# A unit of dense work between the two parts of the second row's scores in stick-breaking attention

## The chip, the cores and the metric

The program runs on one core of a Trainium2 chip. The metric is the device time of one execution in microseconds (us). A core has five engines with queues of their own: TensorE (PE, with its weight loads listed apart as PEld), VectorE (DVE), ScalarE (ACT), GpSimd (POOL) and SyncE (SP), which issues the DMAs here. Each runs its instructions in the order in which they stand, and waits on semaphores for what another engine or a DMA has to deliver.

## The reference

Two layers of a decoder on 1024 tokens of width 1024. Each layer has a mixer of two branches, an output projection and a gated FFN with a short convolution. Branch B of the mixer is the place of the change: strictly causal stick-breaking attention, four heads of 64, swept over blocks of 128 queries.

```python
def block(args):
    q_blk, i = args
    z = jnp.einsum('bhqc,bhkc->bhqk', q_blk, kt).astype(jnp.float32) * scale
    qpos = i * BLOCK + jnp.arange(BLOCK)
    causal = key_pos[None, :] < qpos[:, None]
    log_stay = jnp.where(causal, jax.nn.log_sigmoid(-z), 0.0)
    later = lax.cumsum(log_stay, axis=3, reverse=True) - log_stay
    attn = jnp.where(causal, jnp.exp(jax.nn.log_sigmoid(z) + later), 0.0)
    return jnp.einsum('bhqk,bhkc->bhqc', attn, vt)
...
for l in range(DEPTH):
    h = rmsnorm(x, norm1[l])
    proj = h @ w_in[l]
    ...
    o_a = dilated_mixture(...)
    o_b = stick_breaking_attention(...)
    gates = jax.nn.sigmoid(gate_pre + b_gate[l])
    merged = g_a * (o_a @ w_br[l, :OUT_A]) + g_b * (o_b @ w_br[l, OUT_A:])
    x = x + merged @ w_o[l]
```

## The kernel before

All large products run in f32 accuracy from two reduced parts of each operand (a high part `hi` made by a cast on ACT, a low part `lo` made by a subtraction on DVE), so that one product is three matmuls. The input projections and the gates are computed in pairs with seven block products instead of eight (`pair`, `seven`). Half of one such block product, six matmuls with 512 columns each (lines 1064 to 1066, twice), is a **unit**: a generator hands out one at each step.

The class `Dense` owns these generators. `step()` issues the next unit, with whatever casts, copies and DMAs belong to it; `advance(rate)` adds a rate to the account `due` and calls `step()` for each whole one in it. The function `attend` walks through the attention of the layer in 16 stick items, 4 near items and 16 far items. For each it issues short attention steps one after the other (scores, transpositions, products with the values) and calls `dense.advance(rate)` after each, so that units of dense work stand between the attention's steps on PE. The scores of the next item are issued between the steps of the current one.

A stick item is one head (`u`, 0 to 3, called a **round** below) and one pair of query blocks (`qp`, 3 down to 0). It has two rows of scores, one for each of the two query blocks: `score(0)` and `score(1)`. A row of L keys is worked in parts of at most 512 columns, the last keys first. For each part, two matmuls (lines 649 and 650) write a PSUM bank `z`, and ACT reads it twice: a sigmoid into `beta` (line 716) and one into `stay` (line 717). POOL masks the diagonal block of a row's first part. The pool of banks for `z` has two banks, used in turn, so the part after next has to wait until ACT has read the part. Behind the second row, `scans(2)` puts running products on DVE (lines 736, 738) and their products with `beta` (line 743). Blocks of `beta` are then transposed by PE (line 751, into `sb_t`), split by ACT and DVE (lines 144 and 151, `sbh` and `sbl`) and multiplied with the values (line 764).

Rows with more than 512 keys have two parts. Of second rows these are the ones of `qp` 3 (512 and 512 columns) and `qp` 2 (512 and 256). In the order on PE, a round has the parts z1 (512 columns) and z2 (384) of the first row of `qp` 3, z3 and z4 (512 each) of its second row, z5 (512) and z6 (128) of the first row of `qp` 2, and later z7 (512) and z8 (256) of its second row. There are four rounds in a layer and two layers.

The order of ACT, DVE, POOL and SP is not that of the code alone. A scheduler orders the instructions by priority (the scores' sigmoids and some others are written under `tc.high_priority`), and manual dependencies without a semaphore keep some of them behind others.

Of the kernel before, what the change touches and what calls it, by code (L numbers as in the profile page):

```python
# [63 lines left out]
def trunk_kernel(ctx, tc, x, norm1, w_in, b_gate, w_br, w_o, norm2, w_up, conv_w, conv_b, w_down, norm_f, out, depth=None, probe=None):  # L64
# [63 lines left out]
    def bank(tag, name):  # L128
        return ps.tile([P, 512], F32, tag=tag, name=name)

    def small(name, dtype=F32):
        return sb.tile([P, 512], dtype, tag="pt", bufs=PT, name=name)
# [358 lines left out]
    def table(func, after):  # L491

        junk = sb.tile([P, 1], F32, tag="junk", name="junk")
        return act.activation(junk, after, func, bias=eps[:, 0:1], scale=0.0)
# [153 lines left out]
    def scores(o, qt, ql, k):  # L648
        pe.matmul(o, qt, k, start=True, stop=False, skip_group_check=True)
        pe.matmul(o, ql, k, start=False, stop=True, skip_group_check=True)  # L650

    def parts(src, n, name):

        hi, lo = small(name + "h", F32R), small(name + "l", F32R)
        with tc.high_priority(offset=AHEAD):
            split(hi[:, :n], lo[:, :n], src[:, :n], "is")
        return hi, lo

    def fold(dst, o):

        n = o.shape[-1]
        tmp = small("fold")
        with tc.high_priority(offset=AHEAD):
            act.copy(tmp[0:64, :n], o[64:128, :])
            dve.tensor_tensor(dst, o[0:64, :], tmp[0:64, :n], ALU.add)
# [33 lines left out]
    def stick_item(dense, u, qp):  # L699
        q, k, v = R["slots"][:, qp], R["kv"][:, 0, :], R["kv"][:, 1, :]  # L700
        pr, s = divmod(u, 2)
        rows, st, shared, left = {}, {}, {}, []

        def score(a):
            L = P * (2 * qp + a + 1)
            bt = rows[a] = sb.tile([P, T], F32, tag="p4", bufs=4, name="beta")
            if a == 0:
                st[0] = sb.tile([P, 2, T], F32, tag="xa", bufs=4, name="stay")
            sv = st[0][:, a, :]
            for c1 in range(L, 0, -512):  # L710
                c0 = max(0, c1 - 512)
                w = c1 - c0
                z = bank("s", "z")
                scores(z[:, :w], *(q[:, x, a * P : a * P + P] for x in range(2)), k[:, c0:c1])
                with tc.high_priority(offset=AHEAD):
                    act.activation(bt[:, c0:c1], z[:, :w], AF.Sigmoid)
                    last = act.activation(sv[:, c0:c1], z[:, :w], AF.Sigmoid, scale=-1.0)
                    if (u, qp, a, c0) == (3, 0, 1, 0):
                        one = table(AF.Exp, zero[:, 0:1])
                        tc.add_manual_dep(one.ins, last.ins.name, NO_SYNC, reason="behind")  # L720
                    if c1 == L:
                        pool.affine_select(bt[:, L - P : L], bt[:, L - P : L], [[-1, P]], ALU.is_gt, 0.0, base=0, channel_multiplier=1)
                (SCANS if c1 == L else left).append((shared, bt, sv, c0, c1, L))
            if a:
                SCANS.extend(left)
                dense.rows += 1
                scans(2)

        def scans(most):

            while SCANS and most:
                most -= 1
                _, bt, sv, c0, c1, L = SCANS.pop(0)
                rev = sv[:, c0:c1][:, ::-1]
                if c1 == L:
                    one = dve.tensor_tensor_scan(rev, rev, over[:, HF - (c1 - c0) : HF][:, ::-1], 1.0, ALU.mult, ALU.max)
                else:
                    one = dve.tensor_tensor_scan(rev, rev, zero[:, 0:1].to_broadcast([P, c1 - c0]), sv[:, c1 : c1 + 1], ALU.mult, ALU.add)
                if "dve" in LAST:
                    tc.add_manual_dep(one.ins, LAST["dve"], NO_SYNC, reason="in turn")  # L740
                k0, k1 = max(0, c0 - 1), c1 - 1
                with tc.high_priority(offset=AHEAD):
                    LAST["mult"] = dve.tensor_tensor(bt[:, k0:k1], bt[:, k0:k1], sv[:, k0 + 1 : k1 + 1], ALU.mult).ins.name

        def turn(kb):
            while any(x[0] is shared and x[4] > kb * P for x in SCANS):
                scans(1)
            tp = bank("t", "sb_t")
            todo = [(j, a) for j in range(2) for a in range(2) if kb + j <= 2 * qp + a]
            for c, (j, a) in enumerate(todo):  # L750
                pe.transpose(tp[:, c * P : c * P + P], rows[a][:, (kb + j) * P : (kb + j + 1) * P], ident)
            shared[kb] = parts(tp, len(todo) * P, "sb")
            scans(2)

        def apply(kb):
            first = kb == 2 * qp
            if first:
                shared["o"] = bank("o", "sb_o")[:, :256]
                dense.free[qp] = u + 1
            o = shared["o"]  # L760
            for j in range(2):
                c = P if first and j else 0
                for p in (0, 1):
                    pe.matmul(
                        o[:, c:256],
                        v[:, (kb + j) * P : (kb + j + 1) * P],
                        shared[kb][p][:, 256 * j : 256 * j + 256 - c],
                        start=(first and j == 0 and p == 0),
                        stop=(kb == 0 and j == 1 and p == 1),
                        skip_group_check=True,  # L770
                    )
            if kb == 0:
                out_ = small("ob")[0:64, 0:256]
                fold(out_, o)
                nc.sync.dma_start(obd[64 * s : 64 * s + 64, pr, qp * 256 : (qp + 1) * 256], out_)

        sc = [lambda: score(0), lambda: score(1)]
        return sc, [(lambda kb=kb: turn(kb), lambda kb=kb: apply(kb)) for kb in range(2 * qp, -2, -2)]

# [1439 lines left out]
```

## Time and profile before

| | |
|---|---|
| Time, median of 3 runs | 2613.97 us (2612.62 to 2614.74) |
| Time of the profiled execution | 2614.89 us |
| Its span, first to last instruction | 2613.2 us |
| PE busy | 2602.9 us (100%) |
| PEld busy | 2181.2 us (83%) |
| DVE busy | 2086.4 us (80%) |
| ACT busy | 1353.4 us (52%) |
| POOL busy | 107.4 us (4%) |
| Stick attention, first layer | about 75 to 330 us |
| Stick attention, second layer | about 1366 to 1620 us |

Matmuls overlap in their pipeline and their ends are modelled, so PE counts as busy while it streams at its full rate and also through a short wait. What a wait costs is read from the distance between the starts of matmuls. A row of the time line has the start in us, the duration in us, the engine, the line, the operation and its tiles; in brackets stands idle time of the engine before it, and what ended it.

### The profile page before, as it was taken

Reading aid. Unit: us, or ns where it says so; the run is one execution under the profiler, and the core shown is the slowest. Engines: PE = TensorE matmul, PEld = TensorE weight load, DVE = VectorE, ACT = ScalarE, POOL = GpSimd, SP = SyncE. Lnnn points to the kernel's source line nnn. Section 1 sums busy time; section 2 is a strip of 40 time slices with the busy share of each in tenths; the row PEclk is TensorE's granted clock in tenths of the full one; section 3 lists DMA queues with packets and bytes.
Section 4 is the critical chain, followed back from the end, with each engine's and each line's share of the span. In section 5 each row is a group of like instructions: output and inputs, shape, how many; then the busy total and the mean of one; then the engine's idle time right before and its main releaser. Section 6 shows DMA issues by size and latency. Waiting matters only on the chain.

```text
span 2613.2 us, 36182 instructions
## 1 busy us (share of the span) xinstructions
PE 2602.9 (100%) x12706; PEld 2181.2 (83%) x12706; DVE 2086.4 (80%) x3486; ACT 1353.4 (52%) x2527; POOL 107.4 (4%) x145
## 2 busy tenths in 40 slices
PE   9999999999999999999999999999999999999999
PEld 8888888888888888888888888888888888888887
DVE  7877777785988888897677788777869888889965
ACT  6555666573554555422345555666645555554225
POOL 3000000030000000000000000000300000000000
PEclk9999999999999999999999999999999999999999
DMA  7534578973244454688344436798633344447962
GB/s 255 152 119 133 161 206 218 235 241 97 89 145 161 137 172 135 241 325 312 145 150 142 129 124 186 199 235 230 200 101 121 121 168 139 154 161 263 347 241 107
DMA packets 401123, 470.36 MB, mean 180 GB/s; under 512 B 24468, under 2 KB 315692, under 8 KB 399148
## 3 DMA queue, kind: packets, MB, share of 16 engines
q1 hardware_dynamic: 400220, 465.90, 55.4%
q0 software_dynamic: 704, 2.13, 0.4%
q8 instruction: 101, 1.65, 0.3%
q14 instruction: 82, 0.67, 0.1%
q10 hardware_dynamic: 16, 0.00, 0.0%
HBM read 305.33 MB, written 162.63 MB: 179 GB/s over the span
## 4 chain that ended last, share of the span: by engine, by line
PE 93%; DVE 3%; DMA 2%; ACT 2%; issue 1%; POOL 0%; DVEq 0%; ACTq 0%; POOLq 0%
PE u_a L1064 6%; PE u_a L1065 6%; PE u_a L1066 6%; PE d_ps L1827 5%; PE d_ps L1829 5%; PE d_ps L1828 5%; PE i_a L1064 5%; PE i_a L1066 5%; PE i_a L1065 5%; PE u_c L1064 3%; PE u_c L1065 3%; PE u_c L1066 3%; PE i_c L1064 2%; PE i_c L1066 2%; PE i_c L1065 2%; PE o_ps L185 2%
## 5 line engine op out<-in xcount | busy, mean ns | idle before, releaser
L144 ACT CAST w_hi<-up_a 128x512 fp32r<-128x512 f32 x280 | 174.1, 623 | 276.8 <-DVE up_a L1681 120.6
L151 DVE TENSOR_TENSOR w_lo<-up_a,w_hi 128x512 fp32r<-128x512 f32 x280 | 189.5, 689 | 83.6 <-ACT w_hi L144 83.6
L144 ACT CAST w_hi<-in_a 128x512 fp32r<-128x512 f32 x252 | 156.2, 622 | 166.6 <-PE i_c L1065 37.8
L151 DVE TENSOR_TENSOR w_lo<-in_a,w_hi 128x512 fp32r<-128x512 f32 x252 | 172.8, 688 | 74.5 <-ACT w_hi L144 65.8
L1835 DVE TENSOR_TENSOR x<-x,d_ps 128x512 f32<-128x512 f32 (+1 forms) x228 | 153.6, 675 | 64.9 <-PE d_ps L1829 61.5
L1827 PE MATMUL d_ps<-gd_in,w_hi 128*128 128x512 f32 (+1 forms) x340 | 130.0, 382 | 0.0
L1828 PE MATMUL d_ps<-gd_in,w_hi 128*128 128x512 f32 (+1 forms) x340 | 129.8, 382 | 0.0
L1829 PE MATMUL d_ps<-gd_in,w_lo 128*128 128x512 f32 (+1 forms) x340 | 129.8, 382 | 0.0
L1064 PE MATMUL u_a<-hh,w_hi 128*128 128x512 f32 x320 | 124.5, 389 | 0.0
L1065 PE MATMUL u_a<-hl,w_hi 128*128 128x512 f32 x320 | 124.5, 389 | 0.0
L1066 PE MATMUL u_a<-hh,w_lo 128*128 128x512 f32 x320 | 124.5, 389 | 0.0
L1064 PE MATMUL u_a<-t_hi,w_hi 128*128 128x512 f32 x320 | 124.5, 389 | 0.0
L1065 PE MATMUL u_a<-t_lo,w_hi 128*128 128x512 f32 x320 | 124.5, 389 | 0.0
L1066 PE MATMUL u_a<-t_hi,w_lo 128*128 128x512 f32 x320 | 124.5, 389 | 0.0
L1064 PE MATMUL i_a<-hh,w_hi 128*128 128x512 f32 x288 | 119.2, 414 | 0.0
L1064 PE MATMUL i_a<-t_hi,w_hi 128*128 128x512 f32 x288 | 118.3, 411 | 0.0
L1827 PE MATMUL d_ps<-gd_in,wd 128*128 128x512 f32 (+1 forms) x292 | 113.9, 390 | 0.0
L1066 PE MATMUL i_a<-hh,w_lo 128*128 128x512 f32 x288 | 113.1, 393 | 0.0
L1066 PE MATMUL i_a<-t_hi,w_lo 128*128 128x512 f32 x288 | 113.0, 392 | 0.0
L1065 PE MATMUL i_a<-t_lo,w_hi 128*128 128x512 f32 x288 | 112.9, 392 | 0.0
L1829 PE MATMUL d_ps<-gd_in,wd 128*128 128x512 f32 (+1 forms) x292 | 112.8, 386 | 0.0
L1065 PE MATMUL i_a<-hl,w_hi 128*128 128x512 f32 x288 | 112.8, 392 | 0.0
(389 smaller groups left out, 7826.9 us busy)
## 6 DMA issues: line engine op xcount, KB each, us to landing
gd<-g SPq DMA_DIRECT2D x154, 512.0 KB, 3.2
gd_in<-gd SPq DMA_DIRECT2D x154, 512.0 KB, 5.7
up_a<-in_w_up_dram SPq DMA_DIRECT2D x80, 512.0 KB, 5.5
in_a<-in_w_in_dram SPq DMA_DIRECT2D x72, 512.0 KB, 5.2
wd_raw<-in_w_down_dram SPq DMA_DIRECT2D x22, 1024.0 KB, 11.4
gin<-gs SPq DMA_DIRECT2D x32, 512.0 KB, 4.4
w_raw<-in_w_o_dram SPq DMA_DIRECT2D x64, 256.0 KB, 2.9
gs<-u SPq DMA_DIRECT2D x48, 256.0 KB, 3.0
```

Source lines behind the costliest of these rows:

```text
L144: one = act.copy(hi, src)
L151: two = dve.tensor_tensor(lo, src, f32(hi), ALU.subtract)
L185: pe.matmul(o, lh, rh, start=(first and i == 0), stop=False, skip_group_check=share)
L1064: pe.matmul(o, w[0][:, c], rh, start=(first and i == 0), stop=False, skip_group_check=True)
L1065: pe.matmul(o, w[0][:, c], rl, start=False, stop=False, skip_group_check=True)
L1066: pe.matmul(o, w[1][:, c], rh, start=False, stop=(last and i == 3), skip_group_check=True)
L1827: pe.matmul(o[:, sub], wh[:, c], gh[:, sub], start=(i == 0 and k in (0, 4, 5)), stop=False, skip_group_check=True)
L1828: pe.matmul(o[:, sub], wh[:, c], gl[:, sub], start=False, stop=False, skip_group_check=True)
L1829: pe.matmul(o[:, sub], wl[:, c], gh[:, sub], start=False, stop=(i == m - 1), skip_group_check=True)
L1835: dve.tensor_tensor(x, x, o[:, sub], ALU.add)
```

## The change

When the second row of a stick item has a second part, one unit of dense work is issued right after the row's first part, and the account `due` is lowered by one, so that the next call of `advance` grants one unit less.

```diff
                 (SCANS if c1 == L else left).append((shared, bt, sv, c0, c1, L))
+                if a and c0:
+                    dense.step()
+                    dense.due -= 1.0
             if a:
                 SCANS.extend(left)
                 dense.rows += 1
```

The condition holds in `qp` 3 and `qp` 2 of each round, 16 places in the program. The number of instructions stays the same on every engine. Lines behind the edit have numbers higher by three.

On PE, the third round of the first layer before (z3 is `z_2311`, z4 `z_2317`, z5 `z_2343`, z6 `z_2349`; `i_a` is the bank of the unit):

```order
L649 MATMUL z_2311<-kv_897,slots_898 128x512
L650 MATMUL z_2311<-kv_897,slots_898 128x512
L649 MATMUL z_2317<-kv_897,slots_898 128x512
L650 MATMUL z_2317<-kv_897,slots_898 128x512
L1064 MATMUL i_a_2128<-hh0_194,w_hi_2221 128x512
L1065 MATMUL i_a_2128<-hl0_195,w_hi_2221 128x512
L1066 MATMUL i_a_2128<-hh0_194,w_lo_2222 128x512
...
L649 MATMUL z_2343<-kv_897,slots_898 128x512
L650 MATMUL z_2343<-kv_897,slots_898 128x512
L649 MATMUL z_2349<-kv_897,slots_898 128x128
L650 MATMUL z_2349<-kv_897,slots_898 128x128
```

The three rows of the unit stand there twice. The same place now (z3 is `z_2311`, z4 `z_2328`, z5 `z_2339`, z6 `z_2345`):

```order
L649 MATMUL z_2311<-kv_897,slots_898 128x512
L650 MATMUL z_2311<-kv_897,slots_898 128x512
L1067 MATMUL i_a_2128<-hh0_194,w_hi_2221 128x512
L1068 MATMUL i_a_2128<-hl0_195,w_hi_2221 128x512
L1069 MATMUL i_a_2128<-hh0_194,w_lo_2222 128x512
...
L649 MATMUL z_2328<-kv_897,slots_898 128x512
L650 MATMUL z_2328<-kv_897,slots_898 128x512
L649 MATMUL z_2339<-kv_897,slots_898 128x512
L650 MATMUL z_2339<-kv_897,slots_898 128x512
L649 MATMUL z_2345<-kv_897,slots_898 128x128
L650 MATMUL z_2345<-kv_897,slots_898 128x128
```

The unit that stood between z4 and z5 stands between z3 and z4; z4, z5 and z6 follow each other without a unit. It is so in all four rounds of both layers. In `qp` 2, the unit that stood behind z8 stands between z7 and z8.

On ACT, the same place before (`w_hi` is the high part of a piece of weights, cast from `in_a`):

```order
L716 ACTIVATE beta_2310<-z_2311 128x512
L717 ACTIVATE stay_2290<-z_2311 128x512
L716 ACTIVATE beta_2310<-z_2317 128x512
L717 ACTIVATE stay_2290<-z_2317 128x512
L144 CAST w_hi_2327<-in_a_2118 128x512
L716 ACTIVATE beta_2341<-z_2343 128x512
L717 ACTIVATE stay_2342<-z_2343 128x512
```

and now:

```order
L716 ACTIVATE beta_2310<-z_2311 128x512
L717 ACTIVATE stay_2290<-z_2311 128x512
L144 CAST w_hi_2318<-in_a_2118 128x512
L716 ACTIVATE beta_2310<-z_2328 128x512
L717 ACTIVATE stay_2290<-z_2328 128x512
L716 ACTIVATE beta_2337<-z_2339 128x512
L717 ACTIVATE stay_2338<-z_2339 128x512
```

The cast of a piece of weights has moved with its unit from behind z4's sigmoids to ahead of them. What it reads is written by line 1195 on DVE (line 1198 now). In the second round, a cast (line 144) and a copy of a finished bank (line 1217, now 1220) come to stand between z3's and z4's sigmoids; in the first and the fourth round nothing stands between them.

## Prediction

> **What bounds the kernel now.** I read the page first, then the busy times of the two stick stages, then the waits of the weight loads, and then the time line at each place where a unit moves.
>
> ```profile
> span 2613.2 us, 36182 instructions
> ...
> PE 2602.9 (100%) x12706; PEld 2181.2 (83%) x12706; DVE 2086.4 (80%) x3486; ACT 1353.4 (52%) x2527; POOL 107.4 (4%) x145
> ```
>
> ```profile
> 75.00:330.00 255.00, 254.73 (x1292) 211.96 (x1291) 201.23 (x318) 141.33 (x286) 15.63 (x32) 1.00 0.45 139
> 1366.00:1620.00 254.00, 253.73 (x1288) 211.10 (x1287) 200.17 (x316) 140.75 (x286) 15.65 (x32) 1.00 0.46 140
> 268.00:275.00 7.00, 6.75 (x33) 5.11 (x32) 4.46 (x7) 5.99 (x13) 0.98 (x2) 1.00 0.14 42
> ```
>
> The columns of the second view are stretch, length, then busy PE, PEld, DVE, ACT and POOL with counts, granted clock, share of the DMA engines and GB/s. PE is idle for 10.3 us of the span (2613.2 - 2602.9), and for 0.3 us of either stick stage (255.00 - 254.73). So PE sets the time, and a wait put into its stream, or taken out of it, moves the end by about its own length. In both stages the clock is full.
>
> What PE waits for shows at its weight loads, here over the whole span: who waited for whom, us in total, times, the longest.
>
> ```profile
> PEld z L649 <- ACT stay L717: 4.9, 14, 0.7
> ...
> PEld sb_t L751 <- DVE beta L743: 1.1, 4, 0.3
> ```
>
> The first row is a score's wait for its bank, until ACT has read the part before the last; the second is a transposition's wait for DVE. These 6.0 us are all that a better spread of the scores could give back. The counts of the two stages agree within 1%, so I work out the first layer and take it twice.
>
> **The change, part by part.** It adds and removes no instruction. At 16 places a unit, six matmuls with its casts, moves ahead of the two matmuls of a second part. I go from z3's second matmul to the second matmul of the unit behind z6, and compare that length before and after. The fourth round shows what a part costs that comes too soon:
>
> ```profile
> 268.37 0.39 PE L650 MATMUL z<-kv,slots 128*128 128x512 f32 x1
> ...
> 270.71 0.40 PE L650 MATMUL z<-kv,slots 128*128 128x512 f32 x1
> ...
> 271.35 0.19 PEld L649 LDWEIGHTS z<-kv,slots 128*128 128x128 f32 x1 [0.68 <-ACT stay L717]
> ...
> 271.91 0.39 PE L1065 MATMUL i_a<-t_lo,w_hi 128*128 128x512 f32 x1
> ```
>
> These are z3's and z5's second matmuls, z6's load and the end of the length, which is 3.54 us (271.91 - 268.37). z6 uses z4's bank, and its load sat for 0.68 us until ACT had read z4. From there to the unit's second matmul it is 0.56 us; the unit did not get ahead of z6. The third round:
>
> ```profile
> 206.04 0.40 PE L650 MATMUL z<-kv,slots 128*128 128x512 f32 x1
> ...
> 206.54 0.60 ACT L716 ACTIVATE beta<-z 128x512 f32<-128x512 f32 x1 [0.20 <-PE z L650]
> ...
> 207.03 0.59 ACT L717 ACTIVATE stay<-z 128x512 f32<-128x512 f32 x1
> ...
> 207.96 0.68 DVE L1195 TENSOR_TENSOR in_a<-in_a 128x512 f32<-128x512 f32 x1
> ...
> 208.73 0.62 ACT L144 CAST w_hi<-in_a 128x512 fp32r<-128x512 f32 x1
> ...
> 209.25 0.59 ACT L716 ACTIVATE beta<-z 128x512 f32<-128x512 f32 x1
> 209.27 0.39 PE L1065 MATMUL i_a<-hl,w_hi 128*128 128x512 f32 x1
> ```
>
> Its length is 3.23 us (209.27 - 206.04). At z3 ACT was free: 0.50 us from the part's second matmul to `beta` (206.54 - 206.04), 0.49 to `stay`, 0.59 for `stay`. The bank is empty 1.58 us behind the part's second matmul, and I add 0.05 for the signal to the load: 1.63. The second round has the length of a unit:
>
> ```profile
> 141.60 0.40 PE L650 MATMUL z<-kv,slots 128*128 128x512 f32 x1
> ...
> 142.59 0.40 PE L1064 MATMUL i_c<-t_hi,w_hi 128*128 128x512 f32 x1
> ...
> 142.59 0.59 ACT L717 ACTIVATE stay<-z 128x512 f32<-128x512 f32 x1
> ...
> 143.98 0.40 PE L649 MATMUL z<-kv,slots 128*128 128x512 f32 x1
> ...
> 144.90 0.39 PE L1065 MATMUL i_a<-t_lo,w_hi 128*128 128x512 f32 x1
> ```
>
> Its length is 3.30 us (144.90 - 141.60). A unit takes 1.39 us (143.98 - 142.59), so a matmul 0.23, and z5, z6 and the way to the unit's second matmul 0.92 where nothing waits. A length without any wait is z4 (0.23 and 0.46), a unit and these 0.92: 3.00 us. And the first round:
>
> ```profile
> 78.57 0.39 PE L650 MATMUL z<-kv,slots 128*128 128x512 f32 x1
> ...
> 81.75 0.40 PE L1065 MATMUL i_b<-hl,w_hi 128*128 128x512 f32 x1
> ```
>
> 3.18 us. What the old waits cost is therefore 0.18, 0.30, 0.23 and 0.54, together 1.25 us a layer.
>
> *The new wait in qp 3.* After the change z4's second matmul comes 1.85 us behind z3's (0.23, the unit, 0.23). z4 and z5 wait for nothing: the banks of z2 and z3 are read during the unit. But z6 wants z4's bank after z5 alone, 0.46 us behind z4's second matmul, and gets it after 1.63. All units behind it on PE wait with it. The length becomes 1.85 + 1.63 + 0.56 = 4.04 us where ACT turns to z4 at once. In the first round that is +0.86, in the fourth +0.50; the order shows nothing between z3's and z4's sigmoids there.
>
> *The casts that move with the unit.* In the third round the cast now stands ahead of z4's sigmoids. It reads what line 1195 writes, which stands on DVE behind the same instructions as before and ends at 208.64 (207.96 + 0.68). The cast so starts at 208.73 as before, `beta` of z4 follows 0.52 later at 209.25, and the unit's second matmul 1.69 behind that (0.49 + 0.59 + 0.05 + 0.56): 210.94, +1.67. In the second round a cast and a copy stand there, and their inputs are ready; at 0.52 each behind z3's `stay` (142.59 + 0.50) `beta` starts at 144.13, and the length ends at 145.82, +0.92.
>
> *Transpositions.* Behind that unit, PE comes later by more than the 0.3 us that it waited at most for `beta`. Between nothing and 1.1 us of these waits go in the whole run; I take half, 0.55, since a wait of a load costs PE less than its length (0.68 us cost 0.54 above).
>
> *qp 2.* z7 and z8 use banks that have long been read; none of the 14 waits lies there. I cost these 8 places at nothing. z8's sigmoids come a unit later, and their reader is the last transposition of the item, several units on, which covers them; without that cover the longest wait of a transposition, 0.3 us, would be the price at each, 2.4 in all.
>
> *DVE, POOL, SP.* Low parts and running products change places on DVE by one or two instructions, POOL keeps its order, and on SP some stores and prefetches of later items change places. Nothing of PE waits for a load in this stage, so I cost these at nothing. On ACT and DVE together I bound them from above by one more instruction of 0.52 us ahead of z4 at each of the 8 places, 4.2 us, and from below by the casts not standing in the way (first rival).
>
> Sum: 2 x (0.86 + 0.92 + 1.67 + 0.50) - 0.55 = 7.35 us. The profiled execution, 2614.89 us with a span of 2613.2, becomes 2622.2; it lies 0.9 above the median of the runs, 2613.97, so the forecast is 2621.3 us, 0.28% slower.
>
> A rule that speaks against the change: the view of 268 to 275 us, with the wait of 0.68 us in it, shows a clock of 1.00. The Trainium skill, "TensorE: Matmul & The Clock Gate", section "A second HAM failure mode: psum-queue depth-cycling", says that PE pausing often between groups of matmuls as it cycles through PSUM banks can make the clock gate fall to half speed and back. By the trace the sum stays 7.35; by that rule it would be that of the third rival.
>
> **The rivals.**
>
> *The casts are not in the way.* If ACT reached z4 in time in the second and third rounds too, they would cost 4.04 - 3.30 = 0.74 and 4.04 - 3.23 = 0.81: 2 x 2.91 - 0.55 = 5.3 us, 2619.2 us. Against it stands the order on ACT, and line 1195 at 207.96.
>
> *Not slower.* If z4's bank were free when z6 wants it, only the old waits would go: 2 x 1.25 + 0.55 = 3.05 us, 2610.9 us. It decides at 0.46 us from z4's second matmul to the end of its `stay`; ACT needs 1.58 in the third round.
>
> *The clock falls.* If each new wait, some 1.2 us (1.63 - 0.46), made the two units behind it run at half the clock, 12 x 0.23 = 2.8 us would come on top at each of 8 places: 22 us, 2643 us. The wait of 0.68 us at full clock speaks against it, though the new one is longer. This is how the rule above would act here.
>
> **How the numbers follow.** The change does what it says: the order on PE shows it. The forecast has 0.70, the casts out of the way 0.14, not slower 0.08, the clock 0.02, and 0.06 is left for what I don't see. About 0.2% (5.2 us) is what a measurement of this kernel can tell from no change, a bound at 2619.2 us. Slower by more than that: the forecast, half of the first rival, which ends on the bound, and the clock: 0.79. Within: the other half, not slower, and 0.01 of the rest: 0.16. Faster: 0.05 of the rest, for more than nearly all waits of the stage would have to go. The range goes from 2617.5, below the first rival with all of the transpositions' 1.1 us given back (2618.7) and with the 1 us by which the runs differ, to 2625.5, the forecast with 4.2 us more. Outside it are the second and third rivals, 0.10, and most of the rest.
>
> **What would show it.** The waits of z's load for `stay` fall from 14 to 8, one in each round, and grow from 4.9 us to between 9 and 12, the longest in the third rounds (about 2 us). The length from z3 to the unit behind z6 is about 4.0, 4.2, 4.9 and 4.0 us in the four rounds. No wait stands at z4 or at z8, and the transpositions' 1.1 us shrink. The stick stage is longer by 3 to 4 us in either layer and the rest of the program keeps its length. I am wrong if z6's load waits for less than 0.7 us, if the cast in the third round starts before 208.5, or if the time comes from another stage.

## The result, and the profile after

The changed kernel takes 2621.57 us (median of 8 runs, 2620.63 to 2623.71); the kernel before, run beside it, 2614.27 (8 runs, 2612.62 to 2615.21). The ratio is 1.003, 95% interval 1.0021 to 1.0039: slower by 7.3 us, 0.3 us from the forecast of 2621.3. The profiled execution took 2621.15 us, with a span of 2619.4.

The head of the page, after:

```profile
span 2619.4 us, 36182 instructions
...
PE 2600.7 (99%) x12706; PEld 2181.8 (83%) x12706; DVE 2090.0 (80%) x3486; ACT 1354.9 (52%) x2527; POOL 107.3 (4%) x145
```

The counts are those of before. PE works for 2600.7 us instead of 2602.9 and is idle for 18.7 (2619.4 - 2600.7) instead of 10.3. PE waits longer; it does no more work. The largest row of the waits of the weight loads over the whole span, after (who waited for whom, us in total, times, the longest), shows where:

```profile
PEld z L649 <- ACT stay L717: 12.4, 12, 2.1
```

The wait of the scores for their banks grew from 4.9 us to 12.4, and from at most 0.7 to 2.1. The row of the transpositions that waited for `beta`, 1.1 us before, is gone. The two stick stages by busy time, after (columns as in the prediction):

```profile
75.00:335.00 260.00, 255.94 (x1301) 213.74 (x1300) 202.37 (x320) 142.50 (x288) 16.51 (x32) 1.00 0.44 138
1366.00:1630.00 264.00, 259.94 (x1321) 217.05 (x1320) 205.99 (x329) 143.79 (x292) 14.92 (x32) 1.00 0.46 141
```

PE was idle for 0.3 us of either stage; now it is for 4.1 us of each (260.00 - 255.94, 264.00 - 259.94), and the granted clock is still 1.00. From the first score of the stage to the first score of the near part behind it, the stages took 254.79 and 254.97 us before (the first from 76.16 to 330.94 us) and take 258.26 and 258.29 now (76.15 to 334.41): 3.47 and 3.32 us more. The rest of the span went from 2103.4 to 2102.9 us.

The time line of the first layer, after: in each round z6's load with its wait, and ahead of it what the reading needs.

```profile
78.55 0.39 PE L650 MATMUL z<-kv,slots 128*128 128x512 f32 x1
...
80.37 0.39 PE L650 MATMUL z<-kv,slots 128*128 128x512 f32 x1
...
80.79 0.60 ACT L716 ACTIVATE beta<-z 128x512 f32<-128x512 f32 x1 [0.65 <-PE z L650]
...
81.29 0.59 ACT L717 ACTIVATE stay<-z 128x512 f32<-128x512 f32 x1
...
81.93 0.19 PEld L649 LDWEIGHTS z<-kv,slots 128*128 128x128 f32 x1 [1.14 <-ACT stay L717]
...
82.49 0.40 PE L1068 MATMUL i_b<-hl,w_hi 128*128 128x512 f32 x1
...
141.90 0.19 PEld L649 LDWEIGHTS z<-kv,slots 128*128 128x128 f32 x1 [0.20 <-ACT stay L717]
...
143.82 0.62 ACT L144 CAST w_hi<-in_a 128x512 fp32r<-128x512 f32 x1
...
144.35 0.57 ACT L1220 COPY u<-i_c 128x512 f32<-128x512 f32 x1
...
144.82 0.60 ACT L716 ACTIVATE beta<-z 128x512 f32<-128x512 f32 x1
...
145.96 0.19 PEld L649 LDWEIGHTS z<-kv,slots 128*128 128x128 f32 x1 [1.47 <-ACT stay L717]
...
207.58 0.39 PE L650 MATMUL z<-kv,slots 128*128 128x512 f32 x1
...
209.49 0.68 DVE L1198 TENSOR_TENSOR in_a<-in_a 128x512 f32<-128x512 f32 x1
...
210.25 0.62 ACT L144 CAST w_hi<-in_a 128x512 fp32r<-128x512 f32 x1 [1.10 <-DVE in_a L1198]
...
210.78 0.59 ACT L716 ACTIVATE beta<-z 128x512 f32<-128x512 f32 x1
...
211.91 0.19 PEld L649 LDWEIGHTS z<-kv,slots 128*128 128x128 f32 x1 [2.08 <-ACT stay L717]
...
212.47 0.39 PE L1068 MATMUL i_a<-hl,w_hi 128*128 128x512 f32 x1
...
273.38 0.19 PEld L649 LDWEIGHTS z<-kv,slots 128*128 128x128 f32 x1 [0.23 <-ACT stay L717]
...
274.75 0.19 PEld L649 LDWEIGHTS z<-kv,slots 128*128 128x128 f32 x1 [1.07 <-ACT stay L717]
```

z6 waits in every round: 1.14, 1.47, 2.08 and 1.07 us. In the third round ACT has nothing to do for 1.10 us, because the cast at its head waits for line 1198 on DVE, while z4's sigmoids stand behind it. The waits of 0.20 and 0.23 us, of z3 in the second round and z5 in the fourth, stood in the trace of before with the same lengths. The length from z3's second matmul to the second matmul of the unit behind z6:

| round | before, us | after, layer 1 / 2, us | more, layer 1, us | predicted, us |
|---|---|---|---|---|
| 1 | 3.18 | 3.94 / 3.94 | 0.76 | 0.86 |
| 2 | 3.30 | 4.28 / 4.29 | 0.98 | 0.92 |
| 3 | 3.23 | 4.89 / 4.90 | 1.66 | 1.67 |
| 4 | 3.54 | 3.94 / 3.94 | 0.40 | 0.50 |
| sum | | | 3.80 | 3.95 |

Twice 3.80 is 7.6 us; what the transpositions no longer wait comes off.

### The profile page after: what moved, and what is told of

Its sections match the earlier page's. It is cut to its first block, busy times and chain, and to the rows that moved or that the text cites. A ratio compares the mean times of both kernels' runs of the same rounds, so it can differ in the third digit from the quotient of the medians.

```text
span 2619.4 us, 36182 instructions
## 1 busy us (share of the span) xinstructions
PE 2600.7 (99%) x12706; PEld 2181.8 (83%) x12706; DVE 2090.0 (80%) x3486; ACT 1354.9 (52%) x2527; POOL 107.3 (4%) x145
## 4 chain that ended last, share of the span: by engine, by line
PE 96%; ACT 1%; DMA 1%; DVE 1%; issue 0%; SPq 0%; POOL 0%; DVEq 0%; ACTq 0%
PE u_a L1069 6%; PE u_a L1067 6%; PE u_a L1068 6%; PE d_ps L1830 5%; PE d_ps L1832 5%; PE d_ps L1831 5%; PE i_a L1067 5%; PE i_a L1069 5%; PE i_a L1068 5%; PE u_c L1067 3%; PE u_c L1069 3%; PE u_c L1068 3%; PE i_c L1067 2%; PE i_c L1069 2%; PE i_c L1068 2%; PE o_ps L186 2%
```

## The experiments

The theory: the 8 places in `qp` 3 make all of the difference, because z6 there waits for z4's bank; in the third round the cast ahead of z4's sigmoids makes that wait longer; the 8 places in `qp` 2 cost nothing. The rivals: the time comes from `qp` 2 or from DVE's order, or the cast is not what lengthens the third round, but DVE being late for other reasons. Each kernel was timed beside the kernel before on the same chip, and the differences below are against that.

**Only the places in `qp` 3.** In the changed kernel:

```diff
-                if a and c0:
+                if a and c0 and qp == 3:
```

> The unit moves in qp 3 alone, 8 places; qp 2 is as before. The bank theory (z6 waits for z4's bank, and nothing else costs): the whole difference of the change, 2621 to 2622 us, +7.4 on before, and the waits of z's load for stay as in the changed kernel, 12.4 us in 12. The rival (the changed order of casts, running products and DMAs costs, in all 16 places): about half, 2617 to 2618 us.

Measured: 2622.36 us against 2613.71, ratio 1.0032 (1.002 to 1.0043). The waits of the weight loads in this kernel:

```profile
PEld z L649 <- ACT stay L717: 12.4, 12, 2.1
```

It is the row of the changed kernel, and the lengths are its lengths within 0.02 us (3.94, 4.30, 4.89 and 3.94 us). Half of the edit makes the whole effect. The median lies 0.36 us above the range expected; the two stick stages alone are 6.99 us longer than before, against 6.79 in the changed kernel.

**Only the places in `qp` 2.**

```diff
-                if a and c0:
+                if a and c0 and qp == 2:
```

> The unit moves in qp 2 alone, between z7 and z8; qp 3 is as before. The bank theory: no difference, 2613.3 to 2615.3 us, with 14 waits of z's load of 4.9 us as before. The rival (the changed order costs in all 16 places): 2617 to 2618 us.

Measured: 2613.7 us against 2613.71, ratio 1.0 (0.9991 to 1.0009). The waits of the weight loads in this kernel:

```profile
PEld z L649 <- ACT stay L717: 4.9, 14, 0.7
...
PEld sb_t L754 <- DVE beta L746: 1.2, 4, 0.3
```

Both rows are as before the change within 0.1 us (4.9 us, 14 times; 1.1 us, 4 times). Putting z8 a unit later costs nothing.

**Another bank for z's part in `qp` 3.** The changed kernel, with the second part of each second row there (z4) put into the other pair of banks (those that the transpositions use). z6 then takes z3's bank and need not wait for z4's sigmoids:

```diff
-                z = bank("s", "z")
+                z = bank("t" if a and c1 < L and qp == 3 else "s", "z")
```

> The changed kernel, with z4 (the second part of the second row in qp 3) in a bank of the transpositions' pair instead of the scores'. Order on PE as in the changed kernel. The bank theory: z6 then needs z3's bank, which is read during the unit, so the wait of z6 goes, and of the waits of before only z3's 0.05 us in the second rounds stays: 2614.3 less 2 x 1.2 and less up to 1.1 for transpositions, 2611 to 2612 us; z's load waits for stay under 1 us. The rival (the score's place right ahead of z5 or the order of ACT costs in itself): 2618 to 2622 us.

Measured: 2613.54 us against 2613.71, ratio 0.9998 (0.9989 to 1.0007). The lengths are 2.95, 3.00, 2.95 and 2.95 us, and the only scores that still wait are z3's of the second rounds, 0.20 us in either layer, which stand ahead of the moved unit. The 7.3 us are gone, so the bank was their cause. But it is some 2 us less good than expected. The waits of the weight loads and, behind them, the time line of the third round in this kernel say why:

```profile
PEld sb_t L754 <- DVE beta L746: 2.9, 4, 1.0
...
PEld z L649 <- ACT stay L717: 0.4, 2, 0.2
```

```profile
208.78 0.62 ACT L144 CAST w_hi<-in_a 128x512 fp32r<-128x512 f32 x1 [1.10 <-DVE in_a L1198]
...
209.75 0.66 DVE L151 TENSOR_TENSOR w_lo<-in_a,w_hi 128x512 fp32r<-128x512 f32 x1
...
210.33 0.68 DVE L746 TENSOR_TENSOR beta<-beta,stay 128x512 f32<-128x512 f32 x1
...
211.06 0.20 PEld L754 LDWEIGHTS sb_t<-ident,beta 128*128 128x128 f32 x2 [0.96 <-DVE beta L746]
```

The cast still makes ACT wait for 1.10 us. PE no longer notices it at z6, but comes to the transposition earlier and waits there for `beta`, 0.96 us in this round: 2.9 us in all instead of 1.1. Part of the wait removed came back one step later.

**The same bank in the kernel before**, without the change:

```diff
-                z = bank("s", "z")
+                z = bank("t" if a and c1 < L and qp == 3 else "s", "z")
```

> The kernel before with z4 in a bank of the transpositions' pair and no other change. The bank theory: z4, z5 and z6 no longer wait, every length from z3 to the unit behind z6 becomes 3.0 us: 2.5 to 2.8 us less, 2611.0 to 2611.7 us if the transpositions wait as before (1.1 us), and no less than 2612.5 if their wait grows as in the changed kernel with this bank (2.9 us). The rival (the spread of units matters, not the bank): 2613 to 2615 us.

Measured: 2612.29 us against 2614.1, ratio 0.9993 (0.9985 to 1.0002). No score waits but z3 in the second rounds, and the lengths are 2.95, 3.00, 2.97 and 2.95 us. The waits of the weight loads and the third round's time line in this kernel:

```profile
PEld sb_t L751 <- DVE beta L743: 2.1, 4, 0.6
...
PEld z L649 <- ACT stay L717: 0.4, 2, 0.2
```

```profile
209.46 0.69 DVE L743 TENSOR_TENSOR beta<-beta,stay 128x512 f32<-128x512 f32 x1
...
210.07 0.78 DVE L151 TENSOR_TENSOR w_lo<-in_a,w_hi 128x512 fp32r<-128x512 f32 x1
210.21 0.20 PEld L751 LDWEIGHTS sb_t<-ident,beta 128*128 128x128 f32 x2 [0.58 <-DVE beta L743]
```

By the lengths the old waits cost 0.23, 0.30, 0.26 and 0.59 us, 1.38 us a layer, a little more than the prediction's 1.25. Less came off the time: 1.8 us instead of 2.8 (twice 1.38), since the transpositions' waits grew by 1.0. The median is lower, but the interval holds 1; the two stick stages are 1.80 us shorter. Beside this kernel the one with the change and the bank takes 0.61 us more in these stages (508.56 against 507.95), where the change alone added 6.79. Here `beta` stands ahead of the low part on DVE, in the kernel of the experiment above behind it: there the wait is 0.96, here 0.58 us.

**A unit more in `qp` 3, paid back at z8.** The step is taken without lowering the due time in `qp` 3, and the due time is lowered without a step in `qp` 2. So the unit between z4 and z5 stays, another one stands between z3 and z4, and the one behind z8 is left to later:

```diff
-                    dense.step()
-                    dense.due -= 1.0
+                    if qp == 3:
+                        dense.step()
+                    else:
+                        dense.due -= 1.0
```

> In qp 3 the unit is issued between z3 and z4 without lowering the account, so one stands between z4 and z5 too; in qp 2 the account is lowered and no unit is issued, so the unit behind z8 is the one that is left out. The bank theory: every part has a unit or a read bank behind it, no wait at z4, z5 or z6: 2611 to 2612.5 us. The rival (any unit issued early costs, by casts ahead of z4's sigmoids and low parts ahead of the running products): 2616 us or more, with waits of transpositions or of the products with the values for DVE.

Measured: 2611.2 us against 2613.71, ratio 0.9992 (0.9983 to 1.0001), an interval that still holds 1; the two stick stages are 2.15 us shorter than before. The waits of the weight loads in this kernel, and two rows of its third round:

```profile
PEld z L649 <- ACT stay L717: 1.9, 4, 0.7
```

```profile
207.97 0.62 ACT L144 CAST w_hi<-in_a 128x512 fp32r<-128x512 f32 x1 [1.11 <-DVE in_a L1200]
...
209.63 0.19 PEld L649 LDWEIGHTS z<-kv,slots 128*128 128x128 f32 x1 [0.75 <-ACT stay L717]
```

The same unit at the same place, without taking the unit away that gave ACT its time at z4, leaves 1.9 us of the scores' waits and none of the transpositions' for `beta`. In the first, second and fourth rounds nothing waits but the old 0.20 us of z3 in the second: there it is not the unit between z3 and z4 that costs, but its lack behind z4. In the third rounds z6 still waits for 0.75 us, which had been expected to go: the cast stands ahead of z4's sigmoids as before, and one unit behind z4 does not cover both.

**That, with the other bank.** Both edits together (the last one and the line of the bank).

> The kernel that pays the unit back behind z8, with z4 in a bank of the transpositions' pair besides. What waits for z there are 4 loads, 1.9 us, in the first and third rounds. The bank theory: they go, 1.0 us more of gain, 2610.0 to 2611.0 us. The rival (the wait moves on to a transposition, behind the low part that stands ahead of the running product's product): 2611.2 us as without the bank.

Measured: 2610.45 us against 2614.1, ratio 0.9987 (0.9978 to 0.9996), and the 11 runs lie between 2609.74 and 2611.47. The row that is left of the scores in the waits of the weight loads in this kernel:

```profile
PEld z L649 <- ACT stay L717: 0.4, 2, 0.2
```

The view lists no transposition that waits for `beta`, and of the scores only z3 in the second rounds, 0.20 us each; the four waits of the kernel without the bank had stood in the second and third rounds, not in the first and third as the expectation has it. It beats both kernels, by 3.65 us against the one before; the prediction's rival "not slower" had worked out 3.05 us for all these waits together.

**The change without its third rounds.**

```diff
-                if a and c0:
+                if a and c0 and u != 2:
```

> The change in the first, second and fourth round; the third, where a cast stands ahead of z4's sigmoids, is as before. The theory that the cast makes the third round dearer (1.67 of 3.8 us a layer): 2 x 1.66 us less and the third round's transposition wait of 0.2 us back, 2618.3 to 2618.9 us, with 8 to 10 waits of z's load and the longest 1.4 us. The rival (each round costs alike, 0.95): 2619.5 to 2620 us.

Measured: 2617.88 us against 2614.1, ratio 1.0015 (1.0006 to 1.0024); the lengths are 3.94, 4.30, 3.21 and 3.94 us. The waits of the weight loads in this kernel:

```profile
PEld z L649 <- ACT stay L717: 9.0, 12, 1.5
...
PEld sb_t L754 <- DVE beta L746: 0.6, 2, 0.3
```

Without the two third rounds 3.8 us of the 7.3 are left; by the medians they make 3.5 us, where twice 1.67 was predicted. The time lies 0.4 us below the range expected, which is within the spread of the runs: by the two stick stages the third rounds make 2.93 us (516.55 - 513.62). The lengths alone give 3.4 (twice 4.89 - 3.21), but the transpositions' waits of the third rounds, the second row above, are back. The longest wait is now that of the second rounds, 1.5 us. The count, 12, had been expected to fall to 8 to 10: 4.11 us of a layer's 4.5 are the waits of the other three rounds shown above (1.14, 0.20, 1.47, 0.23 and 1.07), and the sixth is a short one of the third round, which is again as before.

**The third round's cast behind z6's sigmoids.** The changed kernel, with an order on ACT and nothing else: in the third round the cast has to stay behind the sigmoids of z4, the part that follows the moved unit, and in fact comes behind those of z6.

```diff
+        LAST["cast"] = one.ins
...
+                    if (u, qp, a, c0) == (2, 3, 1, 0):
+                        tc.add_manual_dep(LAST["cast"], last.ins.name, NO_SYNC, reason="behind")
```

> The changed kernel, with one dependency more: in the third round the cast of the unit's weights is kept behind z4's stay on ACT (in the order it then stands behind z6's). The theory that the cast, waiting for line 1198 on DVE, holds z4's sigmoids back: z6's load waits 1.2 us there instead of 2.1, the length from z3 to the unit behind z6 falls from 4.9 to 4.0 us, in both layers 1.8 to 1.9 us, 2619.5 to 2620.2 us, and 12.4 us of waits become 10.6. The rival (z4's sigmoids are late for another reason, the cast only fills the time): no difference to the changed kernel, 2621.3 to 2622 us.

Measured: 2619.42 us against 2613.65, ratio 1.0021 (1.0012 to 1.003). The waits of the weight loads and the third round's time line in this kernel (here the numbers of lines behind 144 are higher by one, and those of lines behind the sigmoids by three):

```profile
PEld z L650 <- ACT stay L718: 10.5, 12, 1.5
```

```profile
210.51 0.60 ACT L717 ACTIVATE beta<-z 128x512 f32<-128x512 f32 x1 [0.68 <-PE z L651]
...
211.64 0.19 PEld L650 LDWEIGHTS z<-kv,slots 128*128 128x128 f32 x1 [1.14 <-ACT stay L718]
```

ACT now waits for PE at z4 and not for DVE, z6's load waits for 1.14 us as in the first round instead of 2.08, and the third round's length is 3.95 us instead of 4.89. The prediction's first rival, that the casts are out of the way, is how this round behaves only when the cast is moved by hand. In time this came to 1.5 us less (5.8 us over the kernel before, instead of 7.3), against 1.9 by the two lengths; the intervals of the two ratios overlap, so the difference is not settled by the times alone. The stick stages settle it: they are 1.89 us shorter than in the changed kernel (516.55 - 514.66).

**The two stick stages of every kernel.** Executions of one kernel differ by 1 us and more. The two stages, each from its first score to the first score of the near part and added up, show the effects more sharply, though each row is one profiled execution (differences are of the unrounded times):

| kernel | both stages, us | against before | rest of the span, us |
|---|---|---|---|
| before | 509.75 | | 2103.4 |
| the change | 516.55 | +6.79 | 2102.9 |
| only `qp` 3 | 516.74 | +6.99 | 2105.0 |
| only `qp` 2 | 509.49 | -0.26 | 2102.4 |
| the change, other bank | 508.56 | -1.19 | 2102.3 |
| before, other bank | 507.95 | -1.80 | 2103.2 |
| paid back at z8 | 507.61 | -2.15 | 2101.7 |
| paid back at z8, other bank | 506.43 | -3.32 | 2102.4 |
| without the third rounds | 513.62 | +3.87 | 2104.4 |
| the cast behind | 514.66 | +4.91 | 2104.1 |

The rest of the span, which the edits do not touch, varies by up to 3.3 us from one kernel's execution to another's.

## Why the prediction was right, step by step

*What bounds the kernel.* Right. PE sets the time: 8.4 us more of idle time on PE (18.7 - 10.3), 2.2 less of busy time, 6.2 us more of span.

*The new wait in `qp` 3.* Right in place and mechanism: taking the bank away took the whole effect away. In size it was 0.10 us too dear in the first and fourth rounds. The prediction had z4's second matmul 1.85 us behind z3's and the bank free 1.63 us behind that; measured in the first round are 1.82 (80.37 - 78.55) and 1.56 (81.93 - 80.37). The 0.56 behind it is exact (82.49 - 81.93). The 1.63 were too long at their first term: `beta` starts 0.42 us behind z4's second matmul (80.79 - 80.37), and not 0.50 as at z3, where it had been read. Why these two differ no run shows.

*The casts that move with the unit.* Right. In the third round the cast starts 2.67 us behind z3's second matmul (210.25 - 207.58), against 2.69 before (208.73 - 206.04): it did not come earlier, since line 1198 did not. `beta` of z4 follows 0.53 us later, and +1.66 us was measured for the +1.67 forecast. In the second round the cast and the copy come first, 0.53 and 0.47 us each (144.35 - 143.82, 144.82 - 144.35), and +0.98 was measured for +0.92. The experiment with the cast moved back is what makes the cause shown for the third round. For the second round no run moved the cast and the copy; there the cause rests on the time line.

*Transpositions.* The sign was right, the term probably too small: the whole row of 1.1 us went, and by the stages 0.8 us came off (7.6 - 6.8) where 0.55 was taken. The half did not follow from the reason given for it: at 0.54 for a wait of 0.68, 1.1 us would be worth 0.9. The sum with the measured terms is 7.6 less at most 1.1, so 6.5 to 7.6 us; the medians show 7.3, the two stages 6.8, the two profiled executions 6.3. A term of this size lies at the edge of what single executions can resolve.

*`qp` 2 at nothing.* Right: 0.0 us by itself.

*DVE, POOL and SP at nothing.* Right for the sum: the change in `qp` 3 and the terms above leave nothing over beyond the spread of the runs, and the other stages kept their time. But the order on DVE is not without effect: with the scores' waits gone it goes with how long the transposition waits (0.58 or 0.96 us in the third round).

*The count of the waits.* Wrong: 12, and not 8. The prediction took every old wait to go with the change. Those of z3 in the second rounds, which stands ahead of the moved unit, and of z5 in the fourth, for which the prediction held z3's bank to be read in time, stayed at 0.20 and 0.23 us. At z4 and z8 none stands, as forecast. Their total is slightly over the 9 to 12 us that stood there, 12.4, of which 0.86 are those four old waits; the longest is as forecast (2.1 for about 2).

*The rivals.* "The casts are not in the way" fell with the cast's 1.10 us of waiting, and with the run that moved it. "Not slower" fell at its own deciding point: ACT was done with z4's bank 1.56 us behind the part, not within 0.46. "The clock falls" fell: with waits of up to 2.08 us at z6, the stick stages' clock is 1.00, and lengths behind the waits are those at full speed (0.56 us from the load to the unit's second matmul, as before). The section on psum-queue depth-cycling in the Trainium skill ("TensorE: Matmul & The Clock Gate") tells of a clock that swings where PE idles often between groups of matmuls as it cycles through PSUM banks. This trace has such pauses, twelve times, and shows no swing, with a granted clock of 1.00 in both stages; what shorter distances between them would do no run here shows.

*How close the number came.* That 7.30 us were measured for 7.35 is in part luck. The four lengths were 0.3 us too dear in both layers together (7.9 against 7.6), the transpositions' term was too small by about as much, and the interval of the ratio allows 5.5 to 10.2 us. Place, order of size and the share of each round are what the runs confirm.

## What to carry to other kernels

Filling work that is moved ahead of one part leaves a bare place behind that part, and the price of it can be read off the trace beforehand: the time until the part's bank is read, less the time until it is wanted again. Look also at what moves along on the reading engine: a cast that waits for a third engine holds up everything behind it in order. And a wait that is removed is worth its full length only if nothing comes just behind it; price the next consumer on the path (here the transposition's `beta`) before counting the gain.

## What was not expected of the hardware

A load that waits costs PE less than its wait. The kernel with the change and the other bank has the same order on PE and gives the lengths without a new wait, 2.95 us in the first and third rounds. Against these, z6's 1.14 us lengthened the first round by 0.99 (3.94 - 2.95) and its 2.08 us the third by 1.94 (4.89 - 2.95), so some 0.15 us of each wait cost nothing. The prediction had read 0.54 us as the cost of the wait of 0.68 in the fourth round before, but z5 waited in that length too:

```profile
270.37 0.19 PEld L649 LDWEIGHTS z<-kv,slots 128*128 128x128 f32 x1 [0.23 <-ACT stay L717]
```

The two waits, 0.91 us together, cost 0.59 (3.54 - 2.95), again some 0.16 us less for each. And `beta` could start 0.42 us after the last matmul of a part at z4, 0.49 at z3 of the third round (207.58 to 208.07), with ACT waiting for PE in both.
